# A two-branch recurrent block on one core: z tiles, transposes, norm diagonals, tables, late scans and GLU operands at other places in the written order, and the norm weight products on VectorE

## The chip, the cores and the metric

The kernel runs on one core of one Trainium2 chip. The metric is the device time of one execution in microseconds (us). The engines are called here as in the trace: PE is TensorE, with PEld its weight load; DVE is VectorE; ACT is ScalarE; POOL is GpSimd; SP is SyncE, which here issues nearly all DMAs. A change of under 0.5% of the time counts as no change.

## The reference, cut to what matters

One block of a Griffin-like model, on x of 2048 tokens by 1024 channels in float32.

```python
h = rms_norm(x, norm_w) @ w_in            # u, za | q, f, i, og, zb | gate a, gate b: 5632 columns
# branch A: a diagonal complex state-space layer, 32 groups of 16 channels, 64 states each
ab = exp(lambda * dt)                      # complex
h_t = ab * h_{t-1} + B u_t ;  y = Re(C h) + d*u
y = gelu(y);  y = y * sigmoid(y @ w_glu + b_glu);  ya = y * silu(za)
# branch B: HGRN2, 4 heads of 128, forget gate f with a lower bound, key = 1 - f
S_t = f_t * S_{t-1} + key_t (x) i_t ;  o = q_t S_t ;  o = rms_norm(o * sigmoid(og)) * hnw
yb = o * silu(zb)
m = sigmoid(gate a) * (ya @ w_proj_a) + sigmoid(gate b) * (yb @ w_proj_b)
out = rms_norm(x + m @ w_out, final_norm_w)
```

## The kernel before, in words

The tokens are worked through in two halves of 1024 (called `a` = 0 and 1), each in two blocks of 512 (`b`). All matmuls are in float32 made of two parts: an operand is split into a rounded high part (`split`: ACT line 116) and the rest (DVE line 117), and three products are summed (hi*hi, hi*lo, lo*hi). The big input product `x @ w_in` is done by slices of 256 columns, most of them by a seven-product scheme (`strassen`, lines 405 and on): per product 12 matmuls of 128x512, which is one *step* of the dense work. The seven combinations of x that it needs are made by `xprep`, written to DRAM for reuse (`xo_d`) and, for slices of the second half, loaded again by `x_load` (40 loads).

PE does what the program writes, in that order: the main part is wrapped in a manual schedule for PE. `timed(dense, n, events)` (line 1321) runs the dense work step by step and, at given step numbers, pieces of the small work that the tables `ev` in the main part list: the steps of the HGRN2 heads (`hgrn_core`, `hgrn_fin`), the building of the SSM tables (`ssm_build`), the SSM batches (`ssm_batch`, eight batches of four groups for each half), GELU, the loads for GLU. DVE, ACT, POOL and the DMA queue of SP each work through their instructions in an order that the tile scheduler of the compiler picks from the dependencies and the order of the program; within an engine nothing overtakes.

What the change touches:

- `norm_stats` (line 174): squares of a block on ACT, then an inverse root by Newton steps, 12 tiny DVE instructions (lines 152 to 158). `norm_bcast` (line 193): four diagonals `dg` (DVE line 197), and one matmul `psn` that spreads them over all partitions.
- `later` and `tick` (line 396): the transposes `pt` of V and of the output gate (line 892) are put off by a number of dense steps after their slice is evacuated.
- `hgrn_fin` (line 1043): loads the tile `zy` (silu of z), transposes the head's output (`py`) and multiplies. For the last head of the first half its result is the fourth input of `merge_b` (line 1083), the projection of branch B; that starts with the other three inputs.
- `sn` tiles: a ring of six 128x512 buffers, shared by many loads; a load into a buffer waits until its last reader is done.
- `ssm_batch` (line 729): `psg`, a scan on DVE, then `psy` (lines 810 and 811), both in a PSUM ring `pss` of one buffer. Its first column was copied on POOL (line 803) in the second half.
- `gelu` (line 817): loads y back from DRAM (`yy`), seven passes over ACT and DVE, and writes `ya_d`. `glu_prep` loads `gy` and `gz` from there and from `za_d`; `glu_w` loads the GLU weights; `glu` is the product `pg`.
- `merge` (line 1154): the projection of branch A (`pp`), gates, sum, split into `mh`, `ml`; `out_proj` (line 1212): product `pf`, residual (DVE line 1238), square (ACT line 1240), and for the first 512 output channels the product with the final norm weight (line 1242, on POOL).

Of the kernel before, what the change touches and what calls it, by code (L numbers as in the profile page):

```python
# [31 lines left out]
def hybrid_block(  # L32
# [363 lines left out]
    def later(f):  # L396
        post.append([2, f])
# [331 lines left out]
    def ssm_batch(a, b, wu_pool, vm_pool):  # L729
# [78 lines left out]
        py = pss.tile([128, 4, 128], F32, name=f"psy{a}{b}", tag="pss")  # L808
# [105 lines left out]
    def hgrn_block(a, h, b):  # L914
        o8 = (h % 2) * 8
        n = f"{a}{h}{b}"
        F, Q, Vv, O = (t[b] for t in HT[a, h])
# [11 lines left out]
        for lv in range(9):  # L929
# [73 lines left out]
            yield  # L1003
        ps = psm.tile([128, 512], F32, name=f"pv{n}", tag="psm")
# [38 lines left out]
    def hgrn_fin(a, h, direct=None):  # L1043
        o8 = (h % 2) * 8
        for b in range(NBLK):
# [4 lines left out]
            y = sn(f"zy{a}{h}{b}")  # L1050
            nc.sync.dma_start(y, ft_d["zb", a, h][:, b * 512 : b * 512 + 512])
# [4 lines left out]
            V.tensor_tensor(y, y, ps, op=ALU.mult)  # L1056
            if direct is None:
                nc.sync.dma_start(ft_d["yb", a, h][:, b * 512 : b * 512 + 512], y)
            else:
                direct(b, y)  # L1060
# [95 lines left out]
    def merge(a):  # L1156
# [3 lines left out]
        for jj in range(4):  # L1160
            wn = [None, None]
            for f in range(2):
                j = jj * 2 + f
                fs = slice(f * 128, f * 128 + 128)
                for b in range(NBLK):
                    bs = slice(b * 512, b * 512 + 512)
                    res = []
                    for br in range(2):
                        sg = sn(f"sgl{a}{b}{j}{br}")
                        res.append(sg)  # L1170
                        if w[br] is None:
                            nc.sync.dma_start(sg, ft_d["mb", a, j][:, bs])
                            continue
                        nc.sync.dma_start(sg, ft_d["sg", a, br * 8 + j][:, bs])
                        ps = psd.tile([128, 512], F32, name=f"pp{a}{b}{j}{br}", tag="psd")
                        mac12(ps, w[br], fs, [(YA, YB)[br][a, k, b] for k in range(4)])
                        V.tensor_tensor(sg, sg, ps, op=ALU.mult)  # L1177
                    V.tensor_tensor(res[0], res[0], res[1], op=ALU.add)  # L1178
                    if b == 1:
                        mh = hp.tile([128, 512], F32R, name=f"mh{a}{b}{j}", tag=tags[j])  # L1180
                        ml = hp.tile([128, 512], F32R, name=f"ml{a}{b}{j}", tag=tags[j])
                    else:
                        mh, ml = r2(f"mh{a}{b}{j}"), r2(f"ml{a}{b}{j}")
                    split(res[0], mh, ml)
                    M[b][j] = (mh, ml)
                    if jj < 3 and f == 0 and b == 1:
                        wn = [load_w(wp[0, jj + 1], [128, 4, 256], f"pa{a}{jj + 1}"),
                              load_w(wp[1, jj + 1], [128, 4, 256], f"pc{a}{jj + 1}") if a == 1 else None]
                    yield
            w = wn  # L1190
# [20 lines left out]
    def out_proj(a):  # L1211
# [24 lines left out]
        def add_x(nh, tt, o):  # L1236
# [4 lines left out]
            if nh == 0:  # L1241
                P.tensor_tensor(hh, hh, fw[0], op=ALU.mult)
# [88 lines left out]
    def heads(a, first, every=35, last=22):  # L1331
# [3 lines left out]
        for h in range(4):  # L1335
# [5 lines left out]
            for s in range(4):  # L1341
# [238 lines left out]
```

## Time and profile before

| | before |
|---|---|
| median of 3 runs | 1571.0 us (1570.72 to 1575.9) |
| the profiled execution | 1571.04 us |
| its span, first to last instruction | 1569.0 us |
| PE busy | 1471.6 us, 94% |
| DVE busy | 1098.9 us, 70% |
| ACT busy | 636.9 us, 41% |
| POOL busy | 33.8 us, 2% |
| granted TensorE clock, mean | 0.978 |
| DMA | 368.7 MB, 235 GB/s |

The span is the time between the first and the last instruction; 2.0 us of the execution lie outside it. Busy shares are means over stages that differ. The granted clock is 1.00 at 2.4 GHz and 0.50 at 1.2 GHz.

### The profile page before, as it was taken

To read this page: it belongs to the slowest core of one execution; us is meant where nothing else is said; L and a number is where in the kernel's file an instruction comes from. 1 tells how busy PE (TensorE), PEld (TensorE's weight loads), DVE (VectorE), ACT (ScalarE), POOL (GpSimd) and SP (SyncE) were. 2 spreads that over 40 slices of the span, in tenths; PEclk is the share of its full clock that TensorE was granted. 3 is DMA by queue.
4 is the path that set the end of the run, shared out by engine and by line. 5 is a ranking of instruction groups with operands and counts; after the bars stand their busy time and mean duration, and the time that the engine had idled before them with its cause. 6 is when DMAs were issued, how large, how long until landed. Compare 5 with 4: busy or idle time off the path is not lost.

```text
span 1569.0 us, 21542 instructions
## 1 busy us (share of the span) xinstructions
PE 1471.6 (94%) x7360; PEld 1208.3 (77%) x7360; DVE 1098.9 (70%) x2379; ACT 636.9 (41%) x1385; POOL 33.8 (2%) x52
## 2 busy tenths in 40 slices
PE   7989999999999959989999899999989898899997
PEld 5777688878788748778887778878868787688886
DVE  5798788878788437864676597766648878675535
ACT  6446454554564502233322354333343323441222
POOL 0000000000000000000000000000000021000020
PEclk9999999999999979999999999999999999899999
DMA  9638879977978895775688638777875854764602
GB/s 321 191 98 314 308 266 332 340 265 273 348 277 304 309 327 179 146 252 191 218 273 250 214 125 271 234 245 245 319 256 167 290 184 155 231 204 138 218 14 107
DMA packets 200989, 368.70 MB, mean 235 GB/s; under 512 B 66672, under 2 KB 74864, under 8 KB 200880
## 3 DMA queue, kind: packets, MB, share of 16 engines
q1 hardware_dynamic: 172720, 342.16, 64.4%
q10 hardware_dynamic: 28160, 25.17, 4.6%
q8 instruction: 58, 0.95, 0.2%
q14 instruction: 51, 0.42, 0.1%
HBM read 221.25 MB, written 146.01 MB: 234 GB/s over the span
## 4 chain that ended last, share of the span: by engine, by line
PE 42%; DVE 14%; DMA 10%; ACT 4%; issue 3%; SPq 1%; ACTq 0%; DVEq 0%; POOL 0%; POOLq 0%
PE pd L439 6%; PE pd L441 6%; PE pd L440 6%; DMA yy<-y_d 3%; PE pf L1232 3%; PE pf L1233 3%; PE pf L1234 3%; DMA y_d<-T 2%; PE pp L1085 2%; PE pp L1084 2%; PE pp L1083 2%; ACT ya L825 1%; DVE w L117 1%; DMA rw<-in_wi_dram 1%; PE pg L1084 1%
## 5 line engine op out<-in xcount | busy, mean ns | idle before, releaser
L116 ACT ACTIVATE w<-rw 128x512 fp32r<-128x512 f32 x110 | 68.6, 627 | 89.5 <-PE pd L441 40.5
L1232 PE MATMUL pf<-ho,mh 128*128 128x512 f32 x256 | 101.7, 397 | 2.9 <-ACT mh L116 2.9
L1233 PE MATMUL pf<-lo,mh 128*128 128x512 f32 x256 | 101.0, 394 | 0.0
L1234 PE MATMUL pf<-ho,ml 128*128 128x512 f32 x256 | 100.9, 394 | 0.0
L445 ACT ACTIVATE u<-pd 128x512 f32<-128x512 f32 x80 | 47.5, 593 | 91.8 <-PE pd L441 90.9
L117 DVE TENSOR_TENSOR w<-rw,w 128x512 fp32r<-128x512 f32 x110 | 75.3, 685 | 8.3 <-ACT w L116 7.9
L448 DVE TENSOR_TENSOR u<-u,pd 128x512 f32<-128x512 f32 x80 | 54.8, 686 | 35.7 <-ACT u L445 20.7
L336 PE MATMUL pd<-xh,hw 128*128 128x512 f32 x128 | 52.6, 411 | 8.9 <-ACT hw L116 7.6
L1232 PEld LDWEIGHTS pf<-ho,mh 128*128 128x128 f32 x256 | 49.0, 191 | 13.4 <-ACT mh L116 3.3
L116 ACT ACTIVATE mh<-sgl 128x512 fp32r<-128x512 f32 x32 | 20.2, 632 | 93.8 <-DVE sgl L1178 93.8
L1234 PEld LDWEIGHTS pf<-ho,ml 128*128 128x128 f32 x256 | 48.9, 191 | 10.7 <-DVE ml L117 0.4
L1233 PEld LDWEIGHTS pf<-lo,mh 128*128 128x128 f32 x256 | 48.8, 191 | 10.0
L337 PE MATMUL pd<-xl,hw 128*128 128x512 f32 x128 | 51.4, 402 | 0.0
L338 PE MATMUL pd<-xh,lw 128*128 128x512 f32 x128 | 51.2, 400 | 0.0
L1085 PE MATMUL pp<-yh,lpa 128*128 128x512 f32 x128 | 50.0, 390 | 1.1 <-DVE lpa L117 1.1
L1083 PE MATMUL pp<-yh,hpa 128*128 128x512 f32 x128 | 50.2, 392 | 0.0
L1084 PE MATMUL pp<-yl,hpa 128*128 128x512 f32 x128 | 49.8, 389 | 0.0
L994 DVE TENSOR_TENSOR Q<-Q,t 128x256 f32<-128x256 f32 x96 | 40.5, 423 | 12.7 <-PE sc L969 12.6
L1177 DVE TENSOR_TENSOR sgl<-sgl,pp 128x512 f32<-128x512 f32 x48 | 32.7, 682 | 23.1 <-PE pp L1085 23.1
L958 DVE COPY_PREDICATED s_buf<-masks,sc 128x256 f32<-128x256 uint8 x64 | 32.4, 507 | 23.1 <-PE sc L957 23.0
L952 ACT ACTIVATE KX<-K 128x128 f32<-128x128 f32 x128 | 32.6, 304 | 38.8 <-DVE K L995 29.1
L957 PEld LDWEIGHTS sc<-Q,KX 128*128 128x128 f32 x256 | 38.1, 189 | 9.9 <-DVE s_buf L938 4.1
(916 smaller groups left out, 4459.6 us busy)
## 6 DMA issues: line engine op xcount, KB each, us to landing
wc<-w SPq DMA_DIRECT2D x126, 512.0 KB, 3.4
w<-wc SPq DMA_DIRECT2D x126, 512.0 KB, 4.6
rw<-in_wi_dram SPq DMA_DIRECT2D x44, 512.0 KB, 5.0
sgl<-sg_d SPq DMA_DIRECT2D x48, 256.0 KB, 3.0
sg_d<-u ACTq DMA_DIRECT2D x32, 256.0 KB, 3.9
ro<-in_wo_dram SPq DMA_DIRECT2D x16, 512.0 KB, 4.7
hh<-in_xn_dram SPq DMA_DIRECT2D x32, 256.0 KB, 4.0
out_dram<-hh SPq DMA_DIRECT2D x32, 256.0 KB, 2.3
```

Source lines behind the costliest of these rows:

```text
L116: S.activation(hi, raw, AF.Copy)
L117: V.tensor_tensor(lo, raw, hi.bitcast(F32), op=ALU.subtract)
L439: mm(o, w[:, 0, k], xh, start=(first and k == 0), stop=False, skip_group_check=True)
L440: mm(o, w[:, 0, k], xl, start=False, stop=False, skip_group_check=True)
L441: mm(o, w[:, 1, k], xh, start=False, stop=(k == 3), skip_group_check=True)
L448: V.tensor_tensor(z[key], z[key], ps, op=ALU.add)
L1083: mm(ps, hi[:, k, fs], yh, start=(k == 0), stop=False)
L1084: mm(ps, hi[:, k, fs], yl, start=False, stop=False)
L1085: mm(ps, lo[:, k, fs], yh, start=False, stop=(k == last))
L1232: mm(o, mh[:, ts_], hi, start=(kk == 0), stop=False)
L1233: mm(o, mh[:, ts_], lo, start=False, stop=False)
L1234: mm(o, ml[:, ts_], hi, start=False, stop=(kk == 7))
```

## The change

1. `norm_bcast` is cut in two: `norm_diag` makes the diagonals directly behind `norm_stats`; the matmul stays (for block (1,1) it comes at step 18 instead of 17).
2. `later` puts the transposes off by three ticks instead of two; the head's code reads V and the gate later.
3. In `ssm_batch` the copy of the carried state, and in `out_proj` the product with the norm weight, go from POOL to DVE (8 and 16 instructions).
4. `hgrn_fin` loads both z tiles in a step of its own, for the last head of the first half eight steps ahead of the head's end.
5. In `merge`, the last pair of columns does both tiles of the first token block before those of the second.
6. The step numbers: table building starts at 8 instead of 3; the batches at 64 + 9i instead of 60 + 9.2i; GELU (1,0) goes from the end of the dense part to step 5 of the next part; `glu_prep` (0,0) comes before `glu_w`; the last six batches three steps earlier, with `psy` in another PSUM ring (`psm`); `glu_prep` (1,0) two steps earlier.

```diff
-    def norm_bcast(a, b):
+    def norm_diag(a, b):
         c0 = a * 8 + b * 4
         dg = sn(f"dg{a}{b}")
         for i in range(4):
             V.tensor_scalar(dg[:, i * 128 : (i + 1) * 128], ident, rst[:, c0 + i : c0 + i + 1], None, op0=ALU.mult)
+        return dg
+
+    def norm_bcast(a, b, dg):
         ps = pss.tile([128, 512], F32, name=f"psn{a}{b}", tag="pss")
...
-    def later(f):
-        post.append([2, f])
+    def later(f, steps=3):
+        post.append([steps, f])
...
-    def ssm_batch(a, b, wu_pool, vm_pool):
+    def ssm_batch(a, b, wu_pool, vm_pool, py_pool=(pss, "pss")):
...
-            P.tensor_copy(Hs[:, :, 0], hv)
+            V.tensor_copy(Hs[:, :, 0], hv)
...
-        py = pss.tile([128, 4, 128], F32, name=f"psy{a}{b}", tag="pss")
+        py = py_pool[0].tile([128, 4, 128], F32, name=f"psy{a}{b}", tag=py_pool[1])
...
     def hgrn_fin(a, h, direct=None):
         o8 = (h % 2) * 8
+        y = []
+        for b in range(NBLK):
+            y.append(sn(f"zy{a}{h}{b}"))
+            nc.sync.dma_start(y[b], ft_d["zb", a, h][:, b * 512 : b * 512 + 512])
+        yield
         for b in range(NBLK):
...
-            y = sn(f"zy{a}{h}{b}")
-            nc.sync.dma_start(y, ft_d["zb", a, h][:, b * 512 : b * 512 + 512])
             yield
...
-            for f in range(2):
+            for fb in range(4):
+                f, b = (fb % 2, fb // 2) if jj == 3 else (fb // 2, fb % 2)
...
-                P.tensor_tensor(hh, hh, fw[0], op=ALU.mult)
+                V.tensor_tensor(hh, hh, fw[0], op=ALU.mult)
...
-            for s in range(4):
-                ev.append((t0 + n + 1 + s, lambda f=fins[h]: step(f)))
+            for s in (-8 if a == 0 and h == 3 else 0, 1, 2, 3, 4):
+                ev.append((t0 + n + s, lambda f=fins[h]: step(f)))
...
-        ev += [(2, lambda: norm_stats(1, 0)), (8, lambda: norm_stats(1, 1)), (13, lambda: bcast(0)), (17, lambda: bcast(1))]
+        ev += [(2, lambda: stats(0)), (8, lambda: stats(1)), (13, lambda: bcast(0)), (18, lambda: bcast(1))]
...
-        steps(ev, bg_, [3 + (s * 50) // 42 for s in range(43)])
+        steps(ev, bg_, [8 + (s * 50) // 42 for s in range(43)])
...
-            t = 60 + (i * 92) // 10
+            t = 64 + 9 * i
...
-            if i % 2:
-                ev.append((t + 9, lambda i=i: gelu(i // 8, i // 2 % 4)))
-        steps(ev, glu_w(), [149, 150, 151, 152])
-        steps(ev, glu_prep(0, 0), [150, 151, 152, 153])
+            if i % 2 and i < 9:
+                ev.append((t + 9, lambda i=i: gelu(0, i // 2)))
+        steps(ev, glu_prep(0, 0), [146, 147, 148, 149])
+        steps(ev, glu_w(), [150, 151, 152, 153])
...
         steps(ev, glu_prep(0, 1), [0, 1, 2, 3])
+        ev.append((5, lambda: gelu(1, 0)))
         for i in range(6):
-            g = ssm_batch(1, i + 2, y4, wr4)
-            t = 9 + i * 7
+            g = ssm_batch(1, i + 2, y4, wr4, (psm, "psm"))
+            t = 6 + i * 7
...
-        steps(ev, glu_prep(1, 0), [53, 54, 55, 56])
+        steps(ev, glu_prep(1, 0), [51, 52, 53, 54])
```

No instruction is added on PE and none taken away; 734 of its rows stand at another place. Three places, as rows of the order of an engine (a row's name is that of the tile written, `<-` those read):

SP, before, at the end of the 40 loads of X1 (from `xo_d`), where the first half ends; `zy030` and `zy031` are the z tiles of the last head, `sgb` the gate tiles of `merge_b`:

```order
L288 DMA X124l_5481<-xo_d4_2_134 128x512
L288 DMA X134h_5483<-xo_d4_3_135 128x512
L288 DMA X134l_5485<-xo_d4_3_135 128x512
L1051 DMA zy030_5511<-zb_d0_3_187 128x512
L1051 DMA zy031_5546<-zb_d0_3_187 128x512
L1103 DMA sgb000_5567<-sg_d0_8_152 128x512
L1103 DMA sgb010_5574<-sg_d0_9_153 128x512
```

SP, after: the z tiles stand here, ahead of the loads of branch B's inputs (`yl`) and of all 40 loads of X1:

```order
L375 DMA wc21_1_4987<-w0_21_1_5098 128x1024
L375 DMA wc21_2_4988<-w0_21_2_5145 128x1024
L1052 DMA zy030_5134<-zb_d0_3_187 128x512
L1052 DMA zy031_5136<-zb_d0_3_187 128x512
L1083 DMA yl000_5138<-yb_d0_0_200 128x512
```

SP, after, at the end of the 40 loads:

```order
L291 DMA X124l_5485<-xo_d4_2_134 128x512
L291 DMA X134h_5487<-xo_d4_3_135 128x512
L291 DMA X134l_5489<-xo_d4_3_135 128x512
L1110 DMA sgb000_5567<-sg_d0_8_152 128x512
L1110 DMA sgb010_5574<-sg_d0_9_153 128x512
L1110 DMA sgb001_5581<-sg_d0_8_152 128x512
```

The z tiles went ahead of the 40 loads; the gate tiles `sgb000` and `sgb010` stayed behind them.

DVE, before, at the start of the inverse root (line 152) of block (1,0); `s_buf`, `t000`, `K000` belong to a score level of head 0, `u30_10` and `w0_14_2` to the dense work:

```order
L389 TENSOR_TENSOR rw0_14_1_1415<-rw0_14_1_1415,s20_14_1418 128x4x128
L938 COPY_PREDICATED s_buf0_243<-masks_233,sc000_1_1407 128x2x128
L1000 TENSOR_TENSOR t000_1413<-F000_884 128x256
L448 TENSOR_TENSOR u30_10_1397<-u30_10_1397,pd0_10_3_1355 128x512
L117 TENSOR_TENSOR w0_14_2_1451<-s20_14_1418,w0_14_2_1451 128x512
L995 TENSOR_TENSOR K000_1338<-K000_1338,t000_1413 128x2x64x2
L152 TENSOR_SCALAR small_245<-ssx_248 128x4
L1000 TENSOR_TENSOR t000_1413<-t000_1413 128x128
L153 TENSOR_SCALAR smi_246<-small_245 128x4
```

DVE, after, at the end of the same inverse root, whose steps now stand in one run from line 152 to 158, followed by the diagonals:

```order
L156 TENSOR_TENSOR small_245<-rst_247 128x4
L157 SCALAR_TENSOR_TENSOR small_245<-small_245 128x4
L158 SCALAR_TENSOR_TENSOR rst_247<-small_245,rst_247 128x4
L197 TENSOR_SCALAR dg10_1304<-ident_224,rst_247 128x128 x4
L941 COPY_PREDICATED s_buf0_243<-masks_233,sc000_1_1412 128x2x128
L1003 TENSOR_TENSOR t000_1418<-F000_884 128x256
L998 TENSOR_TENSOR K000_1343<-K000_1343,t000_1418 128x2x64x2
```

The run of the inverse root and the diagonals stand ahead of `s_buf0` of level 1 and of `K000`, where before they followed them and were mixed with other work.

PE, before, at the change from the first slices to the seven-product scheme; `pt` is the transpose of a V/O tile, `pd_6_11` the last product of the old kind, `pd0_10_0` the first of the new:

```order
L337 MATMUL pd_6_11_1133<-xl17_488,hw0_6_11_759 128x512
L338 MATMUL pd_6_11_1133<-xh17_487,lw0_6_11_760 128x512
L892 MATMUL pt0001_1235<-ident_224,vo0001_1191 128x128 x4
L439 MATMUL pd0_10_0_1242<-X000h_815,w0_10_0_1155 128x512
L440 MATMUL pd0_10_0_1242<-X000l_816,w0_10_0_1155 128x512
L441 MATMUL pd0_10_0_1242<-X000h_815,w0_10_0_1155 128x512
```

PE, after, one product further on:

```order
L444 MATMUL pd0_10_0_1235<-X020h_1011,w0_10_0_1155 128x512
L442 MATMUL pd0_10_0_1235<-X030h_1124,w0_10_0_1155 128x512
L443 MATMUL pd0_10_0_1235<-X030l_1125,w0_10_0_1155 128x512
L444 MATMUL pd0_10_0_1235<-X030h_1124,w0_10_0_1155 128x512
L895 MATMUL pt0001_1255<-ident_224,vo0001_1191 128x128 x4
L442 MATMUL pd0_10_1_1262<-X001h_820,w0_10_1_1163 128x512
L443 MATMUL pd0_10_1_1262<-X001l_821,w0_10_1_1163 128x512
```

The transpose went behind the 12 matmuls of the first product.

## Rows read from the trace of the kernel before

**Rows 1.** The page of the profiled execution: its first line, and the busy time of each engine with its share of the span and its instructions.
```profile
span 1569.0 us, 21542 instructions
...
PE 1471.6 (94%) x7360; PEld 1208.3 (77%) x7360; DVE 1098.9 (70%) x2379; ACT 636.9 (41%) x1385; POOL 33.8 (2%) x52
```
**Rows 2.** The waits of TensorE over the whole span, grouped. Columns: engine and line that waited, engine (or DMA) and line that ended the wait, us in total, times, longest.
```profile
PE py L1055 <- DVE zy L1056: 17.3, 1, 17.3
...
PE psn L199 <- DVE dg L197: 7.0, 4, 2.5
PE pg L1083 <- ACT gh L116: 6.8, 2, 5.7
PE pt L892 <- DVE s L448: 5.6, 2, 4.1
PE pt L892 <- ACT vo L886: 4.9, 1, 4.9
PE pd L439 <- ACT u L445: 4.9, 2, 4.2
PE pt L892 <- DVE u L448: 3.5, 3, 2.3
...
PE pg L1084 <- DVE gl L117: 3.2, 5, 1.0
PE pf L1232 <- ACT mh L116: 2.9, 1, 2.9
...
PE psg L772 <- ACT T L812: 2.1, 1, 2.1
...
PE psy L811 <- POOL hh L1242: 1.8, 1, 1.8
PE psy L811 <- issue: 1.7, 1, 1.7
```
**Rows 3.** Chosen stretches. Columns: from and to in us, its length, then busy time and instructions of PE, PEld, DVE, ACT and POOL, the granted TensorE clock, the share of the DMA engines, GB/s.
```profile
565.30:570.44 5.14, 5.14 (x14) 3.88 (x15) 3.26 (x5) 1.15 (x2) 0.00 (x0) 0.50 0.76 263
891.30:894.71 3.41, 2.87 (x9) 2.49 (x10) 3.41 (x7) 2.06 (x3) 0.00 (x0) 0.50 0.11 46
1157.54:1160.95 3.41, 3.41 (x9) 2.65 (x10) 3.38 (x5) 2.39 (x4) 0.00 (x0) 0.50 0.00 0
1358.92:1369.16 10.24, 7.10 (x15) 4.91 (x16) 8.25 (x25) 4.43 (x7) 0.00 (x0) 0.50 0.88 295
1254.00:1358.00 104.00, 96.05 (x452) 79.92 (x450) 78.21 (x167) 34.58 (x66) 15.22 (x12) 0.97 0.55 179
```
**Rows 4.** DVE in order of time, early in the kernel: the sum of the squares of block (0,0), ahead of the steps of its inverse root, and its norm diagonals. Columns: start, us, engine, line, operation, out<-in, shapes, count, and in brackets the idle time before it and what ended it.
```profile
27.05 0.16 DVE L190 TENSOR_TENSOR ssx<-ssh 128x4 f32<-128x4 f32 x1 [4.67 <-ACT xr L184]
...
32.40 0.87 DVE L197 TENSOR_SCALAR dg<-ident,rst 128x128 f32<-128x128 f32 x4
```
**Rows 5.** DVE in order of time, first step of the inverse root of block (1,0) and the step of head 0 before it.
```profile
134.13 0.41 DVE L995 TENSOR_TENSOR K<-K,t 128x256 f32<-128x256 f32 x1
134.47 0.15 DVE L152 TENSOR_SCALAR small<-ssx 128x4 f32<-128x4 f32 x1
```
**Rows 6.** ACT in order of time, the last square of block (1,0).
```profile
133.03 1.06 ACT L188 ACTIVATE xr<-xr 128x1024 f32<-128x1024 f32 x1 [0.16 <-DMA xr<-in_xn_dram]
```
**Rows 7.** PE in order of time, the score matmuls that need that step of head 0.
```profile
135.65 0.62 PE L957 MATMUL sc<-Q,KX 128*128 128x128 f32 x4
```
**Rows 8.** The DMAs that SP issued, first and last of the 40 loads of X1, then the two z tiles and the first four gate tiles.
```profile
528.18 0.38 SPq L288 DMA_DIRECT2D X100h<-xo_d  x1
...
558.31 0.32 SPq L288 DMA_DIRECT2D X134l<-xo_d  x1
558.94 1.04 SPq L1051 DMA_DIRECT2D zy<-zb_d  x2
560.33 2.35 SPq L1103 DMA_DIRECT2D sgb<-sg_d  x4
```
**Rows 9.** DVE in order of time, from the first product with a z tile to the first product with a gate tile.
```profile
564.47 0.69 DVE L1056 TENSOR_TENSOR zy<-zy,py 128x512 f32<-128x512 f32 x1 [22.87 <-DMA zy<-zb_d]
...
567.86 0.69 DVE L1105 TENSOR_TENSOR sgb<-sgb,pb 128x512 f32<-128x512 f32 x1 [0.72 <-PE pb L1085]
```
**Rows 10.** PE in order of time, the first matmul of the second pair of columns of the branch B projection.
```profile
571.02 0.39 PE L1083 MATMUL pb<-Y000h,hpb 128*128 128x512 f32 x1
```
**Rows 11.** DVE in order of time, the one instruction of the table building that waits longest.
```profile
668.28 1.23 DVE L698 TENSOR_TENSOR W<-AR,BB 128x1024 f32<-128x1024 f32 x1 [3.91 <-DMA eh_d<-EH]
```
**Rows 12.** ACT in order of time, the first step of GELU block (1,0).
```profile
1153.69 2.07 ACT L825 ACTIVATE ya<-yy 128x256 f32<-128x256 f32 x4 [5.32 <-DMA yy<-y_d]
```
**Rows 13.** DVE in order of time, in the output projection of the first half.
```profile
1304.10 2.20 DVE L829 TENSOR_TENSOR yy<-yy,ya 128x1024 f32<-128x1024 f32 x1
```
**Rows 14.** POOL in the same stretch.
```profile
1303.46 1.76 POOL L1242 TENSOR_TENSOR hh<-hh,fw 128x512 f32<-128x512 f32 x1 [16.95 <-ACT pf L1240]
```
**Rows 15.** DVE over the whole span, two groups of instructions. Columns: line, engine, operation, out<-in, shapes, count, busy us, mean ns of one, idle time before them.
```profile
L1178 DVE TENSOR_TENSOR sgl<-sgl,sgl 128x512 f32<-128x512 f32 x32 | 22.0, 688 | 2.9 <-DMA sgl<-mb_d 2.3
...
L829 DVE TENSOR_TENSOR yy<-yy,ya 128x1024 f32<-128x1024 f32 x8 | 10.7, 1344 | 0.2
```
**Rows 16.** POOL over the whole span, the group of the norm weight products.
```profile
L1242 POOL TENSOR_TENSOR hh<-hh,fw 128x512 f32<-128x512 f32 x16 | 23.9, 1495 | 243.0 <-ACT pf L1240 216.1 <-DMA ya_d<-ya 26.5
```
**Rows 17.** DVE in order of time, what a step behind the square of a token tile waits.
```profile
1344.97 0.16 DVE L1248 SCALAR_TENSOR_TENSOR small<-small 128x1 f32<-128x1 f32 x1 [0.79 <-ACT pf L1240]
```

More of the change, by code (lines that the diff above doesn't have):

```diff
@@ L916, in hgrn_block @@
         n = f"{a}{h}{b}"
-        F, Q, Vv, O = (t[b] for t in HT[a, h])
+        F, Q = (t[b] for t in HT[a, h][:2])
         K = h2("K" + n, "K")
@@ L1003, in hgrn_block @@
             yield
+        Vv, O = (t[b] for t in HT[a, h][2:])
         ps = psm.tile([128, 512], F32, name=f"pv{n}", tag="psm")
@@ L1055, in hgrn_fin @@
                 nc.tensor.transpose(ch(ps, c), ch(ys, c), ident)
-            V.tensor_tensor(y, y, ps, op=ALU.mult)
+            V.tensor_tensor(y[b], y[b], ps, op=ALU.mult)
             if direct is None:
-                nc.sync.dma_start(ft_d["yb", a, h][:, b * 512 : b * 512 + 512], y)
+                nc.sync.dma_start(ft_d["yb", a, h][:, b * 512 : b * 512 + 512], y[b])
             else:
-                direct(b, y)
+                direct(b, y[b])
             yield
@@ L1161, in merge @@
             wn = [None, None]
-            for f in range(2):
+            for fb in range(4):
+                f, b = (fb % 2, fb // 2) if jj == 3 else (fb // 2, fb % 2)
                 j = jj * 2 + f
                 fs = slice(f * 128, f * 128 + 128)
[L1165 to L1189, printed above, removed]
@@ new lines, in merge @@
+                bs = slice(b * 512, b * 512 + 512)
+                res = []
+                for br in range(2):
+                    sg = sn(f"sgl{a}{b}{j}{br}")
+                    res.append(sg)
+                    if w[br] is None:
+                        nc.sync.dma_start(sg, ft_d["mb", a, j][:, bs])
+                        continue
+                    nc.sync.dma_start(sg, ft_d["sg", a, br * 8 + j][:, bs])
+                    ps = psd.tile([128, 512], F32, name=f"pp{a}{b}{j}{br}", tag="psd")
+                    mac12(ps, w[br], fs, [(YA, YB)[br][a, k, b] for k in range(4)])
+                    V.tensor_tensor(sg, sg, ps, op=ALU.mult)
@@ new lines, in merge @@
+                V.tensor_tensor(res[0], res[0], res[1], op=ALU.add)
+                if b == 1:
+                    mh = hp.tile([128, 512], F32R, name=f"mh{a}{b}{j}", tag=tags[j])
+                    ml = hp.tile([128, 512], F32R, name=f"ml{a}{b}{j}", tag=tags[j])
+                else:
+                    mh, ml = r2(f"mh{a}{b}{j}"), r2(f"ml{a}{b}{j}")
+                split(res[0], mh, ml)
+                M[b][j] = (mh, ml)
+                if jj < 3 and fb == 1:
+                    wn = [load_w(wp[0, jj + 1], [128, 4, 256], f"pa{a}{jj + 1}"),
+                          load_w(wp[1, jj + 1], [128, 4, 256], f"pc{a}{jj + 1}") if a == 1 else None]
@@ L1190, in merge @@
+                yield
             w = wn
@@ L1371, in hybrid_block @@
         norm_stats(0, 0)
+        dg = norm_diag(0, 0)
         g = plain(SL_U + 1, 0, w_u1, u1, wait)
@@ L1376, in hybrid_block @@
         step(g, 2)
-        rb0[0] = norm_bcast(0, 0)
+        rb0[0] = norm_bcast(0, 0, dg)
         run(g)
@@ L1382, in hybrid_block @@
         norm_stats(0, 1)
+        dg = norm_diag(0, 1)
         g = plain(SL_U, 1, w_u0, u0, wait, (psc, "psc"))
@@ L1388, in hybrid_block @@
         step(g, 3)
-        rb0[1] = norm_bcast(0, 1)
+        rb0[1] = norm_bcast(0, 1, dg)
         run(g)
@@ L1420, in bcast, with stats @@
         def bcast(b):
-            rb1[b] = norm_bcast(1, b)
+            rb1[b] = norm_bcast(1, b, dg1[b])
+        dg1 = {}
+        def stats(b):
+            norm_stats(1, b)
+            dg1[b] = norm_diag(1, b)
         ev = heads(0, 3, 35, 18)
-        ev += [(2, lambda: norm_stats(1, 0)), (8, lambda: norm_stats(1, 1)), (13, lambda: bcast(0)), (17, lambda: bcast(1))]
+        ev += [(2, lambda: stats(0)), (8, lambda: stats(1)), (13, lambda: bcast(0)), (18, lambda: bcast(1))]
         xg = chain(*[xprep(1, k, rb1) for k in range(4)])
```

## The prediction

> **What bounds the kernel now.** I read the page first: PE is busy for 1471.6 us of a span of 1569.0 us, DVE for 70% and ACT for 41% [rows 1]. So 97.4 us of the span are PE standing still, and what a change of order can win is of that size. The reader should then look at the grouped waits of PE: twelve groups there hold 61.7 us, none of them a shortage of one engine, each a place where PE's written order comes to an instruction whose input is late [rows 2]. The last thing to read is what a wait costs beside its own length. Behind the longer ones the granted clock is 0.50, the level of 1.2 GHz, for stretches in which PE works 5.14, 2.87, 3.41 and 7.10 us [rows 3]; at the full clock that work would take half, so the waits ahead of them cost 2.6, 1.4, 1.7 and 3.5 us more than they show.
>
> The change adds no PE work and takes none away, so I take each moved step, ask which of these waits it ends, and what is late next.
>
> **Norm diagonals (psn, 7.0 us in 4 waits [rows 2]).** The matmul psn waited for the diagonals, which stood late in DVE's queue; they now follow the inverse root at once. That can give the 7.0 us. But the inverse root and the diagonals have also become one unbroken run on DVE, ahead of work that they used to be mixed with. For block (1,0), the run cannot begin before the last square, which ends at about 134.3 us (133.03 and 1.06, and some 0.2 for reading its sum) [rows 6]; that is also when its first step came before, at 134.47 [rows 5]. Twelve steps of 0.15 to 0.2 us [rows 5] and the diagonals at 0.87 [rows 4] are about 3.2 us, so DVE goes on at about 137.6. The K step of head 0 was finished before the run began (134.13 and 0.41) [rows 5]; now it comes behind it and behind two steps of its own, at about 139, with ACT still to follow, and the score matmuls that need it stood at 135.65 [rows 7]. PE would wait some 4.3 us there, and at half clock afterwards some 1.5. Net for this part: 7.0 - 5.8, and something for the clock behind the waits that go, say +2.5 us. Bounds: -5 (the early loads of x, which now stand behind the rows for the squares, are late by as much as DVE now waits for those, 4.67 [rows 4]) and +8.
>
> **Transposes one dense step later (pt, 4.9 + 5.6 + 3.5 = 14.0 us [rows 2]).** A step is 12 matmuls; in a stretch of mostly such work 452 take 96.05 us of PE [rows 3], 0.21 each, so a step is 2.6 us. Two waits are longer than that (4.9 and 4.1) and keep 2.3 and 1.5; the other four, the rest of 14.0, should go. What is late next is V and the gate for the head, which are read only at its pv step, levels later. So 14.0 - 3.8 = 10.2, and 1.4 of clock behind the wait of 4.1, less for places that move: +10. Bounds 4 and 15.
>
> **z tiles (py, 17.3 us, the longest wait [rows 2]).** The two loads were issued at 558.94, behind 40 loads of X1 that take SP from 528.18 to 558.31 [rows 8]. Now they stand far ahead, and py, the split and the last third of the first four projection tiles can run when the head ends. But PE has four PSUM tiles for this product, and each is freed by a DVE product with a gate tile sgb; these are still issued behind the 40 loads, from 560.33 [rows 8]. With the z tiles out of the way the first is issued at about 558.9. The z tiles took from 558.94 to 564.47 to arrive [rows 8, 9]; the same 5.5 gives 564.4, the DVE product 0.69 [rows 9], and PE begins the next pair of columns at about 565.2 instead of 571.02 [rows 10]. So the gain is +5.8 and not 17.3: the wait moves one pair of tiles on, about 14 us long. Bounds: 2, and 17.3 + 2.6 = 19.9 if the gate tiles do not hold PE up.
> By the Trainium skill's page "DMA: Bandwidth & Descriptors" (Queues, rings and completion order), descriptors are consumed in ring order on each DMA engine; by that a gate tile issued behind 40 loads does not overtake them, which is the 5.8. No row here shows a gate tile issued earlier, and without the rule the term would be up to 19.9.
>
> **GELU (1,0) and the GLU loads.** Near 1150 ACT stood for 5.32 us before GELU's first pass, for a load of y [rows 12]; behind it stood the evacuation that PE wanted, 4.2 of the 4.9 us [rows 2], and 1.7 of clock [rows 3]. With the loads of GLU's operands earlier, the waits of pg for gl (3.2) and the shorter one for gh (6.8 - 5.7 = 1.1) [rows 2] go too: 10.2. GELU does not vanish, it stands in the next part where pg and pp run, and its wait on ACT can come there: I take off 2, +8. Bounds 2 and 11.
>
> **Merge order (pf, 2.9 [rows 2]).** The first product of the output projection needs the splits of the first token block alone, and these are now made first. With about 1.7 of clock, as behind the similar wait at 1157 [rows 3], +4; bounds 1 and 4.6.
>
> **Last batches (psy 1.8 and 1.7, psg 2.1 = 5.6 [rows 2]).** psy no longer shares one PSUM buffer with psg, and the batches come three steps earlier: +4.5, bounds 0 and 7.
>
> **GLU (1,0) (5.7, the long one of pg [rows 2]).** The last GELU is three steps earlier and the loads two; at 2.6 us the step this covers the wait. With the clock 5.7 + 3.5 = 9.2; some of it will stay, as DVE and ACT finish the projection at the same place: +6, bounds 0 and 9.2.
>
> **Norm weight products on DVE.** 16 products at 0.69 [rows 15] are 11.0 us more on DVE, in stages where it has room: 78.21 of 104 us in the first projection [rows 3]. Each also waits for the square of its tile, as a step there does now, 0.79 [rows 17], so 16 times 1.48 = 24 us in all, half of it in that stage: 12 of 25.8 us. On the other side, the POOL version does not leave DVE alone: while POOL worked from 1303.46 for 1.76 us [rows 14], a DVE instruction whose mean is 1.34 [rows 15] took 2.20 [rows 13]. With 16 of them at 1.5 us [rows 16], as much as 14 us of DVE time come back. I cost it at 0; if the room were gone it would be 1.48 a tile.
> The Trainium skill's "GPSIMD Engine Reference" (Specifications) says that POOL's SBUF interfaces are shared with VectorE; the 2.20 against 1.34 agrees. By the rule DVE gains by the move, without it it loses 11; PE has room for both.
>
> **Tables.** The instruction that waited 3.91 us on DVE for a small table [rows 11] keeps its place in the chain and moves five steps on with it: 0, bounds -4 and +4.
>
> **Sum.** 2.5 + 10 + 5.8 + 8 + 4 + 4.5 + 6 = 40.8. Of PE's 97.4 us idle, 35.7 lie in waits that no part aims at; their places shift with everything else, and new ones of the same sort arise where so many rows move. I take a fifth of them, 7, as new; bounds 20 more and 5 fewer. 40.8 - 7 = 34. Against the profiled execution (1571.04, its span 1569.0 and 2.0 around it), which is the median of the runs (1571.0): **1537 us**.
>
> **The rivals.**
> *The long wait goes whole.* If the gate tiles come in time, the z part is 19.9 and not 5.8: 1537 - 14 = 1523. For it: PE waited for nothing else there. Against: the issue times. Chance 0.12.
> *New waits take most of it back.* DVE and ACT are in order, and more runs now stand together: the inverse roots, GELU in the GLU stage, the tables. If each of these three takes its worse bound (-5, 2, -4 for 2.5, 8, 0: 17.5 us) and the pt waits mostly reappear (4 for 10), the sum is 34 - 23.5 = 10, 1561; if half of that, 1549. For it: every such run has a wait at its head now, 4.67, 5.32, 3.91. Chance 0.25 for 1550 to 1570, a third of it within 0.5%.
> *The z tiles block SP.* They take two of six sn buffers eight steps early. If a load behind them on SP (yl) must wait for one of these, SP stands and the 40 loads start later, one for one; then the gate tiles, the end of merge_b and the second half's first products. Held until the head's end, that is some eight steps of 2.6, about 20 us, and the 5.8 is lost as well: 1537 + 5.8 + 20 = 1563. It ends slower than before only from a hold of 28 us, and shows at 36 (1579); a second buffer late in the same way would do that, 1583. Against: other buffers of the ring come free meanwhile. Chance 0.06 for slower.
> The forecast itself, 1526 to 1550, has 0.57.
>
> **The numbers.** The range reaches from just below the first rival to the middle of the second's upper part: 1515 to 1564; the forecast's own is 1526 to 1550. Within 0.5% (about what this kernel's runs can tell from no change) is 1563 to 1579. Faster 0.84, same 0.10, slower 0.06.
>
> **What would show it.** In the profile after: py without a long wait, and instead a PE wait of about 14 us in merge_b that ends with a DVE product with sgb; psn without waits but a sc wait near 136 us; pt waits of 4 us in all; no wait on ACT's u near 1157; no POOL products and DVE about 11 us busier, less what POOL had slowed. The prediction is wrong if the long wait is gone, if SP stands before its 40 loads, or if sc, pd and pg show as many new waits as go.

## The result, and the profile after

| | before | after |
|---|---|---|
| median | 1570.9 us | 1590.8 us (1586.4 to 1593.2, 4 runs) |
| ratio to before | | 1.0124 (95%: 1.0084 to 1.0165) |
| span of the profiled execution | 1569.0 us | 1584.3 us |
| PE busy | 1471.6 us | 1473.2 us |

The kernel became slower by 1.2%. Medians and ratios in this document leave out executions in a slower state of the chip, two of the ten of the transposes alone. The page after (its first line; busy time, share and instructions), which answers to [rows 1]:

```profile
span 1584.3 us, 21509 instructions
...
PE 1473.2 (93%) x7360; PEld 1210.7 (76%) x7360; DVE 1101.9 (70%) x2403; ACT 637.0 (40%) x1385; POOL 4.7 (0%) x28
```

PE does the same work and stands still for 111.1 us instead of 97.4. Its grouped waits (engine and line that waited, what ended it, us in total, times, longest), which answer to [rows 2]:

```profile
PE pd L442 <- ACT u L448: 17.5, 6, 12.5
PE pb L1090 <- DVE sgb L1112: 13.3, 1, 13.3
PE psn L202 <- DVE dg L197: 11.4, 2, 10.0
PE pp L1092 <- DVE lpa L117: 9.9, 1, 9.9
PE pd L442 <- DMA w<-wc: 8.6, 1, 8.6
...
PE pd L442 <- ACT w L116: 5.8, 1, 5.8
...
PE pg L1090 <- ACT gh L116: 3.5, 1, 3.5
PE pg L1091 <- DVE gl L117: 3.0, 3, 1.4
PE pp L1090 <- ACT hpa L116: 2.9, 1, 2.9
```

The reader should see that most of the old list is gone. There is no pt, no py with zy and no pf with mh; psg is away, psy is down to one wait of 0.5, pg gh is 3.5 instead of 6.8. The waits of pg for gl stay (3.0 against 3.2). In place of the others are six single waits of 5 to 13 us that were not there, or were short: u, sgb, psn, lpa, w<-wc and w.

Since PE does the same dense products in the same order, the n-th of them can be compared in both traces. So many us is the kernel after later (+) or earlier (-) than before, at the start of a product; the step is the change since the line above:

```
start before   late    step   what lies between
    38.7       -1.9    -1.9   start
    62.5       +9.2   +11.1   psn of block (0,1)
   112.8       +3.4    -5.8   first transpose
   129.9      +20.3   +16.9   evacuation u, wait at 145.8
   178.5      +10.8    -9.5   old waits of w and psn gone
   531.9      +10.1    -0.7
   573.8       +6.1    -4.0   z tiles, then the gate tile
   799.2       +1.2    -4.9   transposes, tables
   824.2      +11.3   +10.1   w<-wc
   906.8       +7.2    -4.1   old wait of pt at 892 gone
   920.5      +16.5    +9.3   w<-rw
  1108.5      +11.5    -5.0   old waits of sc and pt gone
  1150.3      +19.2    +7.7   waits of pk, pv and po of a head
  1171.2      +13.8    -5.4   u shorter, old waits of pg gone
  1204.4      +25.7   +11.9   lpa
  1233.2      +31.2    +5.5   hpa
  1322.4      +16.8   -14.4   merge, psy, psg
  1365.5      +12.9    -3.9   long wait of pg
  1560.7      +15.4    +2.5
```

The five largest losses, each as the trace after shows it.

**psn of block (0,1), 66 us.** SP in order (start, us, line, DMA, count): the eight xr loads of block (0,0), eight of x, and only behind these the eight xr of block (0,1). Then DVE, which gets their sum and, when the root is done, makes the diagonals:

```profile
18.42 3.76 SPq L183 DMA_DIRECT2D xr<-in_xn_dram  x8
...
27.99 8.28 SPq L216 DMA_DIRECT2D xp<-in_xt_dram  x8
...
39.47 11.19 SPq L183 DMA_DIRECT2D xr<-in_xn_dram  x8
```

```profile
56.48 0.16 DVE L190 TENSOR_TENSOR ssx<-ssh 128x4 f32<-128x4 f32 x1 [6.71 <-ACT xr L184]
...
65.05 0.87 DVE L197 TENSOR_SCALAR dg<-ident,rst 128x128 f32<-128x128 f32 x4
```

The last xr is issued at 50.2, so the sum comes at 56.48 and psn at 65.98, after a wait of 10.0. (From the sum to the diagonals the root takes 8.6 us, as splits of the dense work stand between its steps.)

Two things made the loads late. They start at 39.47, behind the loads of x. And among the eight SP stands from 41.57 to 48.90, until a store of u has landed, which ACT issued. Waits of SP (from 18 to 70 us after, then from 18 to 62 us before):

```profile
SPq L183 <- DMA u_d<-ut: 7.3, 1, 7.3
```

```profile
SPq L491 <- DMA u_d<-ut: 5.8, 1, 5.8
```

Before, such a store held SP at the load of a small constant (line 491), for which PE did not wait; after, it holds the loads of the squares. The program gives the store and the load no data and no buffer in common. In the trace both signal the same semaphore, one of eight that the DMAs of SP and ACT take in turn, and the load waits for the semaphore's last DMA.

**u, 146 us.** ACT in order: the evacuation u that PE needs, before, where it stood ahead of the four squares of block (1,0); then, after, the third and fourth square and u; and DVE after, whose inverse root starts when the last square is done:

```profile
124.19 0.58 ACT L445 ACTIVATE u<-pd 128x512 f32<-128x512 f32 x1
```

```profile
140.07 1.06 ACT L188 ACTIVATE xr<-xr 128x1024 f32<-128x1024 f32 x1 [0.87 <-DMA xr<-in_xn_dram]
...
144.09 1.06 ACT L188 ACTIVATE xr<-xr 128x1024 f32<-128x1024 f32 x1 [2.46 <-DMA xr<-in_xn_dram]
...
145.15 0.58 ACT L448 ACTIVATE u<-pd 128x512 f32<-128x512 f32 x1
```

```profile
145.28 0.17 DVE L152 TENSOR_SCALAR small<-ssx 128x4 f32<-128x4 f32 x1 [3.56 <-ACT xr L188]
```

The squares wait for their loads, and u stands behind the last of them on ACT. PE waited 12.5 us for it.

**w<-wc, 830 us.** SP: a batch's load VM waits, and behind it stand the dense work's weights (w<-wc). DVE beside it waits for E from the same queue:

```profile
814.88 0.42 SPq L743 DMA_DIRECT2D WU<-u_d  x1
822.19 0.32 SPq L744 DMA_DIRECT2D VM<-v_d  x1
...
824.05 1.45 SPq L359 DMA_DIRECT2D w<-wc  x3
```

```profile
826.68 0.69 DVE L758 TENSOR_TENSOR CC<-E 128x512 f32<-128x512 f32 x1 [6.92 <-DMA E<-eh_d]
```

SP stood from 815.3 to 822.2, and the weights, three of them from 824.05, came 8.6 us late for PE. It was not a table that VM waited for: the last store into v_d had landed at 790.6. It was once more a store that ACT issued, of a gate tile, which signals the same semaphore as VM and landed at 822.1. Waits of SP from 806 to 836, and ACT's queue:

```profile
SPq L744 <- DMA sg_d<-u: 6.8, 1, 6.8
```

```profile
820.12 0.33 ACTq L859 DMA_DIRECT2D sg_d<-u  x1
```

**w<-rw, 922 us.** SP: the load of y for a GELU, its result ya (which waits for seven passes on ACT and DVE), and the raw weights behind it; ACT, which splits these:

```profile
903.35 0.37 SPq L824 DMA_DIRECT2D yy<-y_d  x1
917.22 0.32 SPq L835 DMA_DIRECT2D ya_d<-ya  x1
917.64 0.37 SPq L367 DMA_DIRECT2D rw<-in_wi_dram  x1
```

```profile
922.12 0.63 ACT L116 ACTIVATE w<-rw 128x512 fp32r<-128x512 f32 x1 [5.45 <-DMA rw<-in_wi_dram]
```

**lpa, 1215 us.** DVE: a pass of GELU (1,0), the scan of a batch, then lpa, the low part of the projection's weights; and ACT, which made the high part long before:

```profile
1202.38 0.69 DVE L831 TENSOR_SCALAR yy<-yy 128x1024 f32<-128x1024 f32 x1 [0.26 <-ACT yy L830]
...
1209.94 1.60 DVE L792 TENSOR_TENSOR_SCAN T<-r,small,T 128x128 f32<-128x128 f32 x4
...
1214.16 1.23 DVE L117 TENSOR_TENSOR lpa<-rpa,hpa 128x1024 fp32r<-128x1024 f32 x1
```

```profile
1202.25 1.05 ACT L116 ACTIVATE hpa<-rpa 128x1024 fp32r<-128x1024 f32 x1
```

The high part is done at 1203.3. lpa started 10.9 us later, behind GELU (1,0) and the batch, and PE waited 9.9 for it.

### The profile page after: what moved, and what is told of

It reads as the page before. It is cut to its first block, busy times and chain, and to the rows that moved or that the text cites. A ratio compares the mean times of both kernels' runs of the same rounds, so it can differ in the third digit from the quotient of the medians.

```text
span 1584.3 us, 21509 instructions
## 1 busy us (share of the span) xinstructions
PE 1473.2 (93%) x7360; PEld 1210.7 (76%) x7360; DVE 1101.9 (70%) x2403; ACT 637.0 (40%) x1385; POOL 4.7 (0%) x28
## 4 chain that ended last, share of the span: by engine, by line
PE 47%; DVE 12%; DMA 10%; ACT 3%; issue 2%; SPq 1%; ACTq 0%; DVEq 0%
PE pd L442 8%; PE pd L444 7%; PE pd L443 7%; PE pp L1092 2%; PE pp L1090 2%; PE pp L1091 2%; PE pf L1240 2%; PE pf L1239 2%; PE pf L1241 2%; DMA yy<-y_d 1%; PE sc L960 1%; PE pb L1090 1%; DMA rw<-in_wi_dram 1%; PE pb L1091 1%; PE pb L1092 1%
## 5 line engine op out<-in xcount | busy, mean ns | idle before, releaser
L117 DVE TENSOR_TENSOR w<-rw,w 128x512 fp32r<-128x512 f32 x110 | 75.1, 684 | 10.4 <-ACT w L116 10.3
L117 DVE TENSOR_TENSOR lo<-ro,ho 128x512 fp32r<-128x512 f32 (+1 forms) x26 | 20.8, 808 | 35.4 <-PE pf L1240 23.8
```

Of the source, the lines that this page charges most:

```text
L117: V.tensor_tensor(lo, raw, hi.bitcast(F32), op=ALU.subtract)
```

## The experiments

Each is compared with the kernel before on the same chip; theory 1 and 2 are those of the expectation printed above the result. What a run gives against the kernel after is a difference of medians, and the chips are not always the same; taken from the ratios instead, these differences change by up to 2.3 us. The theories behind all of them: (A) the parts that aimed at a wait work as forecast, and the loss comes from what the same moves queued up elsewhere; (B) the parts do not win what was forecast, since what PE waits for stays late.

**Norm diagonals back.** In the kernel after:

```diff
-        dg = norm_diag(0, 0)
...
-        rb0[0] = norm_bcast(0, 0, dg)
+        rb0[0] = norm_bcast(0, 0, norm_diag(0, 0))
...
-            dg1[b] = norm_diag(1, b)
```

> The changed kernel, with the norm diagonals back at their old place (made directly before the matmul psn, block (1,1) at step 17). Theory 1 (the unbroken runs of inverse root and diagonals cost the time in the first 180 us): the waits of PE at 66 us (10.0) and 146 us (12.5) go, the old waits of psn and of the first product of slice 18 near 155 to 178 us (together about 7, with clock 9) come back; the kernel gains about 25 - 9 = 16 us and comes to 1.002 of the kernel before, 1575 us. Theory 2 (the two waits come from the DMAs, which start elsewhere because of the later transposes): both waits stay and the time stays within 5 us of 1591, 1.01 of before.

Measured: 1577.2 us, 1.0050 (1.0029 to 1.0071). Both waits went and the old ones came back: 13.6 us less than after (12 by the ratios). Theory 1.

The same for one half each, (0, b) in the first and (1, b) in the second run:

> The changed kernel, with the norm diagonals of the first half of the tokens alone back at their old place. Theory 1 (the wait at 66 us comes from the loads for the squares of block (0,1), which went behind 13 other loads on SP, and the waits of the two halves are separate): the wait of 10 us at 66 goes, the one of 12.5 at 146 stays: 10 us less, 1581 us, 1.006 of before. Theory 2 (the early delay is hidden by the later one, since both end at a load): the wait at 146 grows by what the one at 66 gives, 1589 to 1592 us.

> The changed kernel, with the norm diagonals of the second half alone back at their old place (block (1,1) at step 17). Theory 1 (separate waits): the wait at 66 stays, the one at 146 (12.5, with clock 14) goes, the old ones between 155 and 178 (7, with clock 9) come back: about 4 us less, 1587 us, 1.010. Theory 2 (shared): 1578 us or less, since the delay at 66 then meets the old waits and is taken up by them.

Measured: 1578.4 us, 1.0048 (1.0026 to 1.0070), and 1586.1 us, 1.0096 (1.0061 to 1.0131). With the first half put back, SP issues the loads of block (0,1) from 28.10 instead of 39.47 and none of them is held, and the wait near 146 stays (waits of PE from 100 to 200 us):

```profile
28.10 5.75 SPq L183 DMA_DIRECT2D xr<-in_xn_dram  x8
```

```profile
PE pd L442 <- ACT u L448: 12.9, 1, 12.9
PE pt L895 <- ACT vo L889: 2.7, 1, 2.7
```

Theory 1 held in both, so the two waits are separate: about 12 us for the first half, and 5 for the second. There the wait of 12.5 goes, and five waits of 1 to 2 us each stand between 141 and 186 us again, as before.

**Tables, batches and GELU (1,0).** Three runs take back the tables alone, GELU (1,0) alone, and all three parts; a fourth the tables and batches without GELU. The first line of the edit is that of the tables, the second of the batches, the rest of GELU:

```diff
-        steps(ev, bg_, [8 + (s * 50) // 42 for s in range(43)])
+        steps(ev, bg_, [3 + (s * 50) // 42 for s in range(43)])
...
-            t = 64 + 9 * i
+            t = 60 + (i * 92) // 10
...
-            if i % 2 and i < 9:
-                ev.append((t + 9, lambda i=i: gelu(0, i // 2)))
+            if i % 2:
+                ev.append((t + 9, lambda i=i: gelu(i // 8, i // 2 % 4)))
...
-        ev.append((5, lambda: gelu(1, 0)))
```

> The changed kernel, with the table building started at step 3 as before (the batches stay at 64 + 9i). Theory 1 (the tables now end too close to the first batch, whose loads hold up SP and DVE near 815 to 830 us): the wait of PE for a weight matrix at 830 us (8.6, with clock 10) goes, and the kernel comes to about 1581 us, 1.006 of before. Theory 2 (that wait belongs to the batches' own places): it stays, and the time is within 3 us of 1591.

> The changed kernel, with GELU (1,0) back at the end of the dense part. Theory 1 (GELU (1,0) in the next part delays the split of the projection's weights on DVE): the wait of pp for lpa at 1215 us (9.9, with clock 11.6) shrinks to under 2, while a wait of about 4 with 1.7 of clock comes back near 1157; net gain about 6 us, 1585 us, 1.009 of before. Theory 2 (the batches that come three steps earlier delay that split): the wait of pp stays above 6 and the kernel is no faster than 1589.

> The changed kernel, with the table building, the places of the ten batches and GELU (1,0) as before. Theory 1 (the new places in the middle cost, by loads and splits that queue up on SP and DVE): the waits of PE at 830 (8.6), 922 (5.8), 1139 (about 6 in all) and 1215 us (9.9) go, with their clock some 34 us; about 10 come back near 1157 to 1171: 1567 us, 0.997 of before. Theory 2 (the waits at 922 and 1139 follow the later transposes, not the batches): only those at 830 and 1215 go, less the 10: 1578 us, 1.005.

> The changed kernel, with the table building and the ten batches at their old places, GELU (1,0) at its new one. Theory 1 (the parts of the middle add): of the 23 us that all three gave back together, GELU (1,0) had 11 alone, so 12 are left for these two: 1579 us, 1.005. Theory 2 (GELU's cost comes from meeting the moved batches): 1570 us or less.

Measured: tables 1584.1 us, 1.0071 (1.0047 to 1.0095), and the wait at 830 is gone: VM is issued at 816.05, without a wait, directly behind WU; GELU 1579.5, 1.0050 (1.0027 to 1.0072); all three 1567.9, 0.9977 (0.9963 to 0.9991); tables and batches 1574.4, 1.0034 (1.0013 to 1.0055). With GELU (1,0) back, the waits of PE from 1140 to 1240 us no longer hold lpa:

```profile
PE pg L1090 <- ACT gh L116: 2.4, 2, 2.3
PE pd L442 <- ACT u L448: 1.4, 1, 1.4
```

All three together cost 23 us, as theory 1 said: 11 for GELU (1,0) when taken back alone, 14 to 16 for tables and batches (between the theories), so they nearly add, with 3 to 5 shared. The tables alone had 7. The wait near 922 for w stays when the tables alone (5.5) or GELU (1,0) alone (5.5) go back and is gone with the batches back, so it comes from the places of the batches, which were not taken back alone; nor was the order of the GLU loads. The wait for lpa stays with tables and batches back (11.0) and goes with GELU (1,0) back, so it is GELU's.

**z tiles alone,** on the kernel before (parts `hgrn_fin` and `heads` of the diff):

> The kernel before, with the early load of the two z tiles alone. Theory 1 (the gate tiles behind the 40 loads hold PE up): the wait of 17.3 us for the z tile becomes one of about 13 to 14 for a gate tile one pair of columns later, and the kernel gains about 5.8 us: 1565 us, 0.996 of before. Theory 2 (PE would not wait for the gate tiles in this order): no long wait, 1551 us, 0.987.

Measured: 1564.5 us, 0.9960 (0.9941 to 0.9979), 6 to 7 us less than before. The wait of 17.3 has become this one, as theory 1 said:

```profile
PE pb L1086 <- DVE sgb L1108: 13.9, 1, 13.9
```

**Gate tiles ahead of the 40 loads,** with the z tiles:

```diff
+    def sgb_load(a, j):
+        SGB[a, j] = y4(f"sgb{a}{j}")
+        nc.sync.dma_start(SGB[a, j], ft_d["sg", a, 8 + j])
...
+        ev += [(122, lambda: sgb_load(0, 0)), (122, lambda: sgb_load(0, 1))]
```

> The kernel before, with the early z tiles, and with the gate tiles of the first pair of columns of merge_b loaded ahead of the 40 loads of X1 (into two buffers of 128x1024 that are idle there). Theory 1 (the 13.9 us that PE waits with the z tiles alone are the queue on SP and nothing else): the wait goes, with its clock 16 us: 1549 us, 0.986 of before, and 0.990 of the z tiles alone. Theory 2 (the next tiles in the queue, the gate tiles of the second pair or the weights, are as late): the wait moves on once more and the gain is under 5: 1560 us or more.

Measured: 1568.2 us, 0.9980 (0.9965 to 0.9995), nothing won over the z tiles alone (3 to 4 us more). Theory 2 held: the wait of 13.9 became two, 4.8 for the next gate tiles and 8.5 for the first weights of the second half (w), while the DMA engines are busy for 0.95 of the stretch:

```profile
PE pd L439 <- ACT w L116: 10.7, 2, 8.5
...
PE pb L1086 <- DVE sgb L1117: 4.8, 1, 4.8
```

```profile
528.00:605.00 77.00, 61.43 (x271) 49.59 (x270) 25.74 (x48) 13.55 (x36) 0.54 (x3) 0.91 0.95 327
```

(Columns of the last as in [rows 3].) These weights are issued around and behind the last 16 loads of X1:

```profile
583.37 0.48 SPq L364 DMA_DIRECT2D rw<-in_wi_dram  x1
...
597.18 1.01 SPq L364 DMA_DIRECT2D rw<-in_wi_dram  x2
```

So the next run issues them ahead of those 16 loads, with the z and gate tiles early as above:

```diff
-        x_load(5)
-        x_load(6)
         d1 = strassen(1, s1)
         step(d1)
+        x_load(5)
+        x_load(6)
```

> The kernel before, with the early z tiles, the gate tiles ahead of the 40 loads, and the first weights of the second half issued ahead of the last 16 loads of X1. Theory 1 (the 8.5 us that PE then waited for these weights were again the queue on SP): the wait goes and about 9 us are won over 1568: 1558 us, 0.992 of before. Theory 2 (the stretch from 528 to 605 us is bound by the bytes of the DMAs, at a busy share of 0.95): the wait comes back behind X1 or the next weights, 1565 us or more.

Measured: 1556.5 us, 0.9907 (0.9881 to 0.9933). The weights are issued at 577.0 and 580.5, the wait for them is gone, and the kernel is 15 us under the kernel before:

```profile
577.02 0.50 SPq L364 DMA_DIRECT2D rw<-in_wi_dram  x1
580.50 0.49 SPq L364 DMA_DIRECT2D rw<-in_wi_dram  x1
```

So it was order in the queue and not the bytes: the DMA engines are still busy for 0.93 of the same stretch, at 315 GB/s. The order had to be mended for three sets of loads, z, gate and weights. (The weights early without the other two were not tried; neither the kernel before nor the z tiles alone shows a wait for them.)

**Transposes.** With two steps in the kernel after, and with three in the kernel before:

```diff
-    def later(f, steps=3):
+    def later(f, steps=2):
```

> The changed kernel, with the transposes put off by two steps as before. Theory 1 (each transpose that comes a step later saves its wait): the pt waits come back, about 14 us and some clock, and the time goes to about 1602 us, 1.020 of before. Theory 2 (the later transposes gave back what they saved, by a wait of the head's code): no change, 1589 to 1593.

> The kernel before, with the transposes put off by three steps instead of two and nothing else. Theory 1 (the saved waits were real, and only the other parts hid them): the pt waits, 14 us, shrink to about 4 and nothing else grows: 1561 us, 0.994 of before. Theory 2 (what the transposes wait for is late for all that stands behind it, so that the wait only changes its place by one product): pt shrinks, but waits of sc, pv, po or pd of the same length come behind: 1569 to 1573 us.

Measured: 1590.4 us, 1.0126 (1.0091 to 1.0160), as the kernel after, theory 2; and alone 1564.5 us, 0.9955 (0.9932 to 0.9977), 7 us less, between the theories and nearer theory 1 (no profile of it is read here). In the first of them, from 100 to 200 us, the pt wait is back and the wait for u is shorter by half of it:

```profile
PE pd L442 <- ACT u L448: 9.8, 1, 9.8
PE pt L895 <- ACT vo L889: 5.1, 1, 5.1
```

PE arrives there later, and what it waits for has its own time, set by loads: the wait for u ends at 146.4 here and at 145.8 in the kernel after.

**The tail alone,** on the kernel before:

> The kernel before, with the parts of the tail alone: merge order, the products and copies on DVE, psy in its own PSUM ring, the last six batches three steps and the GLU loads of (1,0) two steps earlier. Theory 1: the waits of pf (2.9), psy and psg (5.6) and most of the long one of pg (5.7) go with their clock, about 11 us: 1560 us, 0.993. Theory 2 (11 us more on DVE, each product behind a square of ACT, delay the projection): gain under 4, 1568 or more.

Measured: 1562.0 us, 0.9955 (0.9924 to 0.9986): 10 us by the medians, 7 by the ratio, nearer theory 1. The waits of pf, psy and psg are gone or under 1 us, the long one of pg is 3.6, and one of 2.7 for hpa is new. The parts of the tail were not run one by one.

**The parts that paid,** in the kernel after with norm diagonals, tables, batches, GELU (1,0) and the order of the GLU loads as before, and the gate tiles early; then with the first weights early too; then with the transposes at two steps:

> The changed kernel without the parts that cost: norm diagonals, tables, batches of the middle, GELU (1,0) and the order of the GLU loads as before; kept are the later transposes, the early z tiles, the products on DVE, the merge order, the last batches with their own PSUM ring and the GLU loads of (1,0); and the gate tiles ahead of the 40 loads. Theory 1 (the parts add up): 1567 of the middle put back, less 14 for the norm diagonals, less 16 for the gate tiles: 1537 us, 0.978 of before. Theory 2 (they share waits and do not add): 1550 us or more.

> The changed kernel without the parts that cost, with the gate tiles early (as in the run of the kept parts, 1559.5 us), and the first weights of the second half ahead of the last 16 loads of X1. Theory 1: 9 us less than that, 1550 us, 0.987 of before. Theory 2 (bound by bytes): 1557 us or more.

> The fastest kernel so far (1551 us: the parts that paid, the gate tiles and the first weights early), with the transposes put off by two steps as before. Theory 1 (the later transposes save about 5 us where no fixed wait stands behind them, as alone on the kernel before): 1556 us, 0.990 of before. Theory 2 (no more than the shift of waits): 1550 to 1552 us.

Measured: 1559.5 us, 0.9912 (0.9883 to 0.9942); **1551.1 us, 0.9865 (0.9827 to 0.9904)**; 1552.2 us, 0.9885 (0.9853 to 0.9916). The first came 22 us above its 1537, theory 2; the gate tiles' 16 are missing there, as in the run with them and the z tiles. The second is the fastest of all, 1.35% under the kernel before (theory 1), with two moves that the change did not have, gate tiles and weights; what is left of the waits at the places of this study:

```profile
PE pd L442 <- ACT u L448: 8.4, 4, 4.8
...
PE pb L1090 <- DVE sgb L1121: 4.4, 1, 4.4
...
PE pd L442 <- ACT w L116: 3.2, 1, 3.2
```

In the third, the pt waits are 4.9 and 4.2 (2.6 and 2.5 in the second):

```profile
PE pt L895 <- ACT vo L889: 4.9, 1, 4.9
PE pt L895 <- DVE s L451: 4.2, 1, 4.2
```

At the products that start at 107.5 and 878.3 us it is 5.5 and 4.1 us later than the second run, and 33 and 11 us on it is 1.0 and 0.2 earlier: each saving was given back at once. What is left of it, 1.1 us between the medians and 3 by the ratios, lies within both intervals, which are too wide to rule out all of theory 1's 5 us.

Of the theories behind all of them, (A) fits the norm diagonals, GELU (1,0), tables and batches; (B) fits the transposes in the kernel after and the gate tiles.

## Why the prediction was wrong

1537 us was forecast (1515 to 1564), 1590.8 came.

- **Norm diagonals (+2.5 forecast; a loss of 12 to 14).** The step that failed is that only DVE was costed. In the first half the text looked at loads of x late behind the squares, and gave them a bound of 5 by a wait that DVE had before. What came late was the next block's squares, whose loads went behind eight loads of x on SP and there behind a store of u: the runs show 12 (f1). In the second half the run of the inverse root did wait for the last square, but the price, 5.8, was taken for the wrong instruction: not the score matmuls behind DVE, but the evacuation u behind the squares on ACT, 12.5 and its clock.
- **Transposes (+10; 7 alone, nothing in the kernel after).** The waits went, all 14 us. The step "what is late next is V and the gate" failed: PE came earlier to waits whose end is set by loads and by other engines (e6, f4). Why 7 us remain alone on the kernel before (e9) is not explained.
- **z tiles (+5.8).** Right: 6 us (e4), and the wait of 13.3 on a gate tile, which the order of SP had told. PE went on at 575.50, 10.3 us later than forecast, and it had come to the place 10.1 late.
- **GELU (1,0) and GLU loads (+8; a loss of 11 for GELU).** The waits from 1157 to 1171 shrank, 4.2 of u to 2.6, and 3.0 of pg to nothing there; those for gl stand at a later GLU product instead, near 1391 (2.8 of 3.0). The step "I take off 2" failed: GELU's passes stand on DVE, with a batch, ahead of lpa, which the product pp needs; the price was a wait of 9.9 and its clock.
- **Tables and batches (0, bounds 4; a loss of 14 to 16).** The largest miss. The text followed one wait of DVE to its new place, gave the moved ten batches no term, and did not look at the queue of SP. There a batch's load behind a store of ACT (6.8 us), and the store of a GELU's result (13.4 us of SP), hold up the weights of the dense work.
- **Merge, last batches, GLU (1,0) (+14.5; 7 to 10).** Right in kind (e10). Part was given back near 1258, at a wait for hpa (2.9).
- **Norm weight products (0).** Right as far as DVE's time shows it; they were not run alone. 16 products at 0.69 us are 11 us, yet DVE's busy time grew by 3.0, and the instruction that took 2.20 beside POOL [rows 13] now has a mean of 1.22, against 1.34 [rows 15]:

```profile
L1249 DVE TENSOR_TENSOR hh<-hh,fw 128x512 f32<-128x512 f32 x16 | 11.0, 685 | 1.5 <-ACT pf L1247 1.5
...
L832 DVE TENSOR_TENSOR yy<-yy,ya 128x1024 f32<-128x1024 f32 x8 | 9.8, 1224 | 0.2
```

- **New waits (7; some 75, the positive steps of the table, clock included).** The rival "new waits take most of it back" had the mechanism, with a chance of 0.25, but its worst sum, 1561, was made from bounds as narrow as the terms, so the loss lay outside every case it had. The rival that ended slower named SP, rightly, but the wrong load: the z tiles block nothing.

## What to carry to other kernels

A step that is moved takes its DMAs along; in a kernel with one load queue, look in the order of that queue at what stands behind each moved load that itself has to wait, before looking at any engine. Ask the profile what such a load waits for: twice here it was not its own data but a store issued by another engine. A wait of the busiest engine is worth its length only if what stands behind it is not tied to a load or a slower chain: with several waits in a row on one queue, mending the first gave only a part (z tiles: 7 us), the second nothing until the third was mended too (12 us between the medians). When many moves of one diff share the time, undo them one by one: here they added up to within a few us, and the moves that paid, with the gate tiles and weights early, gave 1.35%.

## What the runs showed of the hardware

While POOL worked on two SBUF operands, a DVE instruction took 1.6 times the mean of its kind (2.20 against 1.34), and with 16 such POOL products and 8 small copies moved to DVE its busy time grew by 3.0 us instead of 12, in the kernel after and in the run of the tail alone (1101.9 in both, 1098.9 before). The Trainium skill's "GPSIMD Engine Reference" (Specifications) says that GpSimd's SBUF interfaces are shared with VectorE; the 2.20 against 1.34 agrees.
